# First x rows, w1 and w2 rounded to bf16 by the loading DMA; whole form rows stored; three plain h pairs

## The chip, the cores and the metric

One core of a Trainium2 chip runs the whole computation. Its engines are named as in the profile: PE (TensorE, matmuls) with PEld (its weight loads), DVE (VectorE), ACT (ScalarE), POOL (GpSimd) and SP (SyncE, which here only issues DMAs; the profile calls its queue SPq). SP and POOL each issue DMAs to a queue of their own: q1 (hardware_dynamic) is SP's, q0 (software_dynamic) is POOL's; both are served by the same 16 DMA engines. The metric is the device time of one execution in microseconds; lower is better.

## The reference

```python
y = np.matmul(x, w1) + b1          # x: 16x512x768, w1: 768x3072
y = 0.5 * y * (1.0 + erf(y / np.sqrt(2.0)))
out = np.matmul(y, w2)             # w2: 3072x768, all float32 in and out
```

The 16 x 512 rows of x are one list of 8192 rows.

## The kernel before

**Tiling.** The rows are taken in passes of 768 (the last pass has 512); a pass is two halves of 384 rows (`HW`). The inner sizes are K = 768 = 6 blocks of 128 (`KC`), H = 3072 = 24 blocks (`HC`) and N = 768. All matmuls run in bf16 and sum in float32 in PSUM. Blocks h and h + 12 form an "h pair" j (`HP` = 12 pairs).

**Seven products in place of eight.** Both layers use a Strassen-Winograd-like scheme with seven products M1 to M7 on 2x2 blocks. The first layer's matrix operand comes in seven "forms" per h pair: two of them are plain blocks of w1 (M3, M4), five are sums or differences (M1, M5, M2, M6, M7). For one pair they take 7 x 3 x 128 = 2688 bf16 per partition, one `SLOT`. They are too large for SBUF beside the rest, so they lie in a DRAM tile `w1f`, one row of slots per pair, and are read back into a ring of seven slots, `w1t` (`RING` = 7), in every pass after the first. The second layer's seven forms of w2 stay in SBUF (`w2t`, seven places per pair, in the order M3, M4, M1, M5, M2, M6, M7).

**Pass 0** computes the first layer the plain way (`plain(hc, half)`: six matmuls of 384 columns and one gelu on ACT), because the forms of w1 don't exist yet. Pass 1 still does its first `PLAIN` = 4 h pairs in the plain way, 24 matmuls for each, and the other eight with `product1`, 21 matmuls for each. Later passes do all twelve pairs with `product1`.

**Loading.** The inputs are float32. SP loads the first six x tiles (`load_x0`), w1 in nine pieces (`load_w1`, list `W1G`) and w2 in twelve (`load_w2`, list `W2P`) into scraps of other tiles (`xft`, `st`, `ot`, `tt`, the end of `w2t`). DVE, ACT and POOL then round each to bf16: `cast_x0` and `cast_w1`. `turn_x0` transposes an x tile on PE and copies it from PSUM into `xt`. `make_w2(j, part)` reads the float32 scrap of pair j: DVE writes five sums into `w2t`, POOL copies the two plain blocks. The lists `ORDER` and `USER` interleave loads and casts so that a scrap is free before it is loaded again.

**Order.** Every instruction is issued through `inorder`, so each engine runs its own list in the order of the program; engines meet through semaphores. In pass 0 the list of DVE after the first layer is: sums of gelu rows for the second layer (`gsum`), between them the sums of the last three w2 pairs (`late_w2`), and then the evacuations of the second layer (`evacuate`, lines 117-135). PE runs through M3 and M4 of the second layer pair by pair for all three row blocks, then M1, M5, M2, M7, M6 of each block (`rest`).

**Forms.** `make_w1` makes the five sums for one pair on DVE (four instructions) into a scrap in `tt` or `st` and SP stores them to `w1f`. `store_raw` stores the two plain blocks of all pairs in two DMAs with pieces of 768 bytes. Pass 0 calls `make_w1` in `forms(1)` after some of the second layer's products; pass 1 calls the rest between its plain pairs, two after each. `load_raw_slots` issues the first loads of the ring as soon as the raw w1 below a slot is used up.

**Tiles used twice.** `tt` is both the place of form scraps and the place to which `product1` evacuates (`tj = tt[:, j % 2]`); `xft` holds sums of x (`sum_x`). The x of the next pass comes through POOL's queue (`prepare_x`: a DMA that rounds to bf16, into one of three `xb` buffers) and a transposing DMA on SP's queue.

Of the kernel before, what the change touches and what calls it, by code (L numbers as in the profile page):

```python
# [12 lines left out]
P = 128  # L13
# [17 lines left out]
def kernel(  # L31
# [23 lines left out]
    PLAIN = 4  # L55
# [47 lines left out]
    def add(dst, a, b):  # L103
        inorder(nc.vector.tensor_tensor(out=dst, in0=a, in1=b, op=ALU.add))  # L104
# [147 lines left out]

    def make_w2(j, part):
        s = s2[j]
        b11, b12, b21, b22 = s[:, 0, :NB], s[:, 0, NB:], s[:, 1, :NB], s[:, 1, NB:]
        f = w2t[:, j]
        if part == 0:
            sub(f[:, WF["M3"], :], b22, b12)
            sub(f[:, WF["M4"], :], b11, b21)
            copy("pool", f[:, WF["M5"], :], b22)  # L260
            copy("pool", f[:, WF["M2"], :], b11)
        else:
            add(f[:, WF["M1"], :], b11, b22)
            add(f[:, WF["M6"]:WF["M7"] + 1, :], s[:, :, :NB], s[:, :, NB:])

    def raw(j):
        return w1t[:, j * RAW:(j + 1) * RAW].rearrange("p (hh kh c) -> p hh kh c", hh=2, kh=2)

    stf = st[:].rearrange("p a b c -> p (a b c)")
    ttb = tt[:].rearrange("p a b c -> p (a b c)").bitcast(BF16)  # L270
    made = 0
    FORMS0 = 7

    def make_w1():
        nonlocal made
        j = (made + PLAIN) % HP
        a = raw(j)
        area, n = (ttb, made % 3) if made < FORMS0 or made >= FORMS0 + 4 else (stf, made - FORMS0)
        made += 1
        s = area[:, n * 5 * KH * P:(n + 1) * 5 * KH * P].rearrange("p (f c) -> p f c", f=5)  # L280
        add(s[:, 0, :], a[:, 0, 0, :], a[:, 1, 1, :])
        add(s[:, 1:3, :], a[:, :, 0, :], a[:, :, 1, :])
        sub(s[:, 3, :], a[:, 0, 0, :], a[:, 1, 0, :])
        sub(s[:, 4, :], a[:, 1, 1, :], a[:, 0, 1, :])
        dma(nc.sync, out=w1f[j].rearrange("p (f c) -> p f c", f=7)[:, 2:, :], in_=s)

    def store_raw(f, blk):
        src = w1t[:, :HP * RAW].rearrange("p (j b c) -> p j b c", j=HP, b=4)[:, :, blk, :]
        dma(nc.sync, out=w1f[:].rearrange("j p (f c) -> p j f c", f=7)[:, :, f, :], in_=src)

    def plain(hc, half):
        pool, nm = ((ps_x, "psx"), (ps_y, "psy"))[half]
        hh, j = divmod(hc, HP)
        py = pool.tile([P, 512], FP32, name=nm)
        for kc in range(KC):
            o = ((j * 2 + hh) * KC + kc) * P
            inorder(nc.tensor.matmul(out=py[:, :HW], lhsT=w1t[:, o:o + P], rhs=xt[:, kc, half, :],  # L297
                                     start=(kc == 0), stop=(kc == KC - 1)))
        inorder(nc.scalar.activation(out=g[:, hc, half, :], in_=py[:, :HW], func=ACTF.Gelu,  # L299
                                     bias=b1t[:, hc:hc + 1], scale=1.0))  # L300
# [14 lines left out]
    late = w2t[:].rearrange("p a b c -> p (a b c)")[:, 8 * 7 * NB:]  # L315
    xftf = xft[:].rearrange("p a b c -> p (a b c)")

    def words(ap, first, count):
        return ap[:, 2 * first:2 * (first + count)].bitcast(FP32)

    otw = ot[:].rearrange("p a b -> p (a b)")
    ttw = tt[:].rearrange("p a b c -> p (a b c)")
    W1G = [(0, 1, words(xftf, 0, 768)), (1, 2, words(xftf, 768, 1536)), (12, 3, words(stf, 0, 2304)),
           (3, 3, otw), (15, 3, words(late, 0, 2304)), (6, 3, words(xftf, 0, 2304)),
           (18, 3, words(stf, 0, 2304)), (9, 3, otw), (21, 3, words(xftf, 0, 2304))]
    pa, pb, pc = ttw[:, :1536], ttw[:, 1536:3072], words(stf, 2304, 1536)
    pd, pe = words(xftf, 0, 1536), otw[:, :1536]
    W2P = [words(late, 2304, 1536), words(late, 3840, 1536), pa, pb, pc, pa, pb, pe, pc, pd, pa, pb]

    def load_x0(n):  # L330
        s = words(late, n * K, K)
        dma(nc.sync, out=s, in_=xf[n * P:(n + 1) * P, :])
        return s

    def cast_x0(s, engine):
        xb = xbp.tile([P, K], BF16, name="xb")
        copy(engine, xb[:], s)
        return xb

    def turn_x0(n, xb, e1):  # L340
        pt = ps_z.tile([P, KC, P], BF16, name="psz")
        for kc in range(KC):
            inorder(nc.tensor.transpose(out=pt[:, kc, :], in_=xb[:, kc * P:(kc + 1) * P], identity=ident[:]))  # L343
        half, c0 = place(HW, n)
        copy(e1, xt[:, :, half, c0:c0 + P], pt[:])

    s1, s2 = {}, {}

    def load_w1(n):
        h0, nh, area = W1G[n]  # L350
        s1[n] = area.rearrange("p (kc c) -> p kc c", kc=KC)
        dma(nc.sync, out=s1[n], in_=w1r[:, :, h0 * P:(h0 + nh) * P])

    def cast_w1(n, engines):
        h0, nh, _ = W1G[n]
        for i in range(nh):
            hh, j = divmod(h0 + i, HP)
            o = (j * 2 + hh) * KC * P
            copy(engines[i], w1t[:, o:o + KC * P].rearrange("p (kc c) -> p kc c", kc=KC),
                 s1[n][:, :, i * P:(i + 1) * P])  # L360

    def load_w2(j):
        s2[j] = W2P[j].rearrange("p (hh n) -> p hh n", hh=2)
        dma(nc.sync, out=s2[j], in_=w2r[:, j, :, :])

    def group(n):
        h0, nh, _ = W1G[n]
        for hc in range(h0, h0 + nh):
            plain(hc, 0)
            plain(hc, 1)  # L370


    xs = [load_x0(n) for n in range(3)]
    load_w1(0)
    b1s = words(stf, 2304, P)[:HC, :]
    dma(nc.sync, out=b1s, in_=b1.rearrange("(hc p) -> hc p", p=P))
    load_w1(1)
    xs += [load_x0(n) for n in range(3, 6)]
    load_w1(2)
    load_w1(3)  # L380
    ident32 = words(stf, 2432, P)
    make_identity(nc, ident32)
    nc.gpsimd.tensor_copy(out=ident[:], in_=ident32)
    xbs = [cast_x0(xs[n], e) for n, e in enumerate(("dve", "act", "dve"))]
    for n, e in enumerate(("act", "dve", "dve")):
        turn_x0(n, xbs[n], e)
        busy(1)
    cast_w1(0, ["act"])
    tb = ps_z.tile([P, 512], FP32, name="psz")
    inorder(nc.tensor.transpose(out=tb[:, :HC], in_=b1s, identity=ident32[:HC, :HC]))  # L390
    copy("act", b1t[:], tb[:, :HC])
    cast_w1(1, ["dve", "pool"])
    for n in range(3):
        plain(n, 0)
    for n, e in enumerate(("dve", "act", "dve")):
        turn_x0(n + 3, cast_x0(xs[n + 3], "act" if n == 1 else "dve"), e)
    for n in range(3):
        plain(n, 1)

    pool3 = ["pool"] * 3  # L400
    engines = {2: ["pool", "dve", "pool"], 3: ["dve", "pool", "dve"], 4: ["pool", "dve", "pool"]}
    ORDER = ["a4", "b0", "a5", "b1", "b2", "a6", "b3", "a7", "b4", "a8",
             "b5", "b6", "b7", "b8", "b9", "b10", "b11"]
    USER = {"a5": "a1", "a6": "a2", "a7": "a3", "a8": "a5", "b5": "b2", "b6": "b3", "b7": "a7",
            "b8": "b4", "b9": "a8", "b10": "b5", "b11": "b6"}
    waiting = ["a2", "a3"]

    def process(what):
        k = int(what[1:])
        if what[0] == "a":  # L410
            cast_w1(k, engines.get(k, pool3))
        elif k < 9:
            make_w2(k, 0)
            make_w2(k, 1)

    for what in ORDER:
        while USER.get(what) in waiting:
            process(waiting.pop(0))
        (load_w1 if what[0] == "a" else load_w2)(int(what[1:]))
        waiting.append(what)  # L420
    for what in waiting:
        process(what)
    for n in range(2, 9):
        group(n)
    late_w2 = [lambda: make_w2(9, 0), lambda: make_w2(10, 0), lambda: make_w2(11, 0),
               lambda: make_w2(9, 1), lambda: make_w2(10, 1), lambda: make_w2(11, 1)]
    store_raw(WF["M3"], 0)
    store_raw(WF["M4"], 3)


    for p, (r0, w) in enumerate(pairs):
# [43 lines left out]
        else:  # L475
            js = list(range(PLAIN if p == 1 else 0, HP))
            if p == 1:
                for j in range(PLAIN):
                    for hc in (j, HP + j):
                        plain(hc, 0)  # L480
                        plain(hc, 1)
                    for _ in range(2):
                        if made < HP:
                            make_w1()
                    load_raw_slots(j + 1)
                for k in range(5):
                    sum_x(k, w)
# [33 lines left out]
        def load_raw_slots(plain_done=0):  # L521
            nonlocal nload
            free = 0
            while nload < RING:
                k = (nload + FIRST) % RING
                need = {j for j in range(HP) if j * RAW < (k + 1) * SLOT and (j + 1) * RAW > k * SLOT}
# [29 lines left out]
        if ns > 2:  # L556
# [6 lines left out]
            rest(2, "M7", forms(1) if later else xsums(4))  # L563
# [31 lines left out]
```

## Time and profile before

| what | value |
|---|---|
| median of 3 runs | 901.2 us (901.19 to 901.29) |
| profiled execution | 901.6 us |
| its span, first to last instruction | 899.8 us |
| PE busy | 890.4 us, 99% of the span, 5556 matmuls |
| DVE / ACT / POOL busy | 619.8 / 379.4 / 102.8 us |
| granted TensorE clock | 0.999 |
| first layer of pass 0 runs without a gap from | 16.36 us |
| its last matmul ends, second layer begins | about 60.2 us |
| plain pairs of pass 1 | 101.70 to 117.30 us |

The profiled execution is 0.4 us above the median, and 1.8 us of it lie outside the span. "Busy" counts an engine's instructions only; a matmul's duration includes its time in the pipeline, so the pace of matmuls is read from how far apart they start: twelve of 384 columns take 1.95 us, 0.1625 us each. A name like `tt<-w1t` reads "writes tt, reads w1t"; x12 means that twelve instructions are merged.

### The profile page before, as it was taken

How to read it: one execution, taken by the hardware profiler on the slowest of the kernel's cores; microseconds unless marked ns; L12 is line 12 of the kernel's file. 1: busy time of each engine (PE TensorE's matmuls, PEld its weight loads, DVE VectorE, ACT ScalarE, POOL GpSimd, SP SyncE). 2: the span in 40 equal slices, each digit the busy share in tenths (PEclk: the TensorE clock that was granted, in tenths of full speed). 3: DMA queues.
4: the chain of work that ended last, by engine and by line, in shares of the span. 5: the costliest groups of instructions: out<-in, count | busy, mean ns of one | idle time of the engine just before them, and what ended most of it. 6: DMA issues, size and time to landing. Idle time of an engine off the chain costs nothing.

```text
span 899.8 us, 14338 instructions
## 1 busy us (share of the span) xinstructions
PE 890.4 (99%) x5556; PEld 542.7 (60%) x5556; DVE 619.8 (69%) x1080; ACT 379.4 (42%) x600; POOL 102.8 (11%) x167
## 2 busy tenths in 40 slices
PE   7999999999999999999999999999999999999998
PEld 4656666666666666666666666666666666666774
DVE  3798956677667676766776676767667766767665
ACT  4541264057207603740572176038306711850460
POOL 2871100010110011000101100110001011000000
PEclk9999999999999999999999999999999999999999
DMA  9998986356717554672557266545726682662411
GB/s 327 385 350 174 316 312 192 106 154 206 185 60 205 200 133 113 213 183 90 171 198 176 74 208 202 133 118 194 180 88 184 204 157 87 205 201 88 153 37 71
DMA packets 92952, 158.23 MB, mean 176 GB/s; under 512 B 50877, under 2 KB 68309, under 8 KB 92885
## 3 DMA queue, kind: packets, MB, share of 16 engines
q1 hardware_dynamic: 79732, 122.32, 43.3%
q0 software_dynamic: 13152, 35.00, 15.2%
q8 instruction: 43, 0.70, 0.3%
q14 instruction: 25, 0.20, 0.1%
HBM read 123.88 MB, written 33.42 MB: 175 GB/s over the span
## 4 chain that ended last, share of the span: by engine, by line
PE 98%; DMA 1%; SPq 0%; ACT 0%; DVE 0%; issue 0%
PE psx L203 21%; PE psy L203 21%; PE psx L160 18%; PE psy L160 18%; PE psz L203 7%; PE psz L160 6%; PE psy L297 3%; PE psx L297 3%; DMA xft<-in_w_dram 1%; SPq L73 0%; ACT g L299 0%; PE psz L343 0%; ACT xb L97 0%; DVE w1t L99 0%; DVE xt L99 0%
## 5 line engine op out<-in xcount | busy, mean ns | idle before, releaser
L160 PEld LDWEIGHTS <-w1t 128*128 128x128 bf16 x2436 | 238.4, 98 | 144.4
L203 PEld LDWEIGHTS <-st 128*128 128x128 bf16 x1920 | 187.9, 98 | 124.1
L97 ACT COPY x<-psx 128x384 f32<-128x384 f32 (+1 forms) x148 | 67.5, 457 | 265.2 <-PE psx L203 191.2
L160 PE MATMUL psx<-xft,w1t 128*128 128x384 bf16 (+1 forms) x696 | 147.2, 320 | 0.0
L160 PE MATMUL psy<-xft,w1t 128*128 128x384 bf16 (+1 forms) x696 | 147.2, 320 | 0.0
L168 ACT ACTIVATE g<-tt,b1t 128x768 bf16<-128x768 f32 (+1 forms) x116 | 106.0, 914 | 80.5 <-DVE tt L107 80.5
L203 PE MATMUL psx<-w2t,st 128*128 128x384 bf16 x768 | 135.3, 326 | 0.0
L203 PE MATMUL psy<-w2t,st 128*128 128x384 bf16 x768 | 135.3, 326 | 0.0
L104 DVE TENSOR_TENSOR q<-x,psy 128x384 f32<-128x384 f32 (+1 forms) x148 | 80.2, 543 | 53.7 <-ACT x L97 38.6
L172 ACT ACTIVATE g<-tt,b1t 128x768 bf16<-128x768 f32 (+1 forms) x116 | 105.8, 912 | 22.8 <-DVE tt L107 22.8
L97 ACT COPY z<-psz 128x384 f32<-128x384 f32 (+1 forms) x148 | 69.3, 468 | 98.7 <-PE psz L203 55.8
L203 PEld LDWEIGHTS <-g 128*128 128x128 bf16 x768 | 75.1, 98 | 49.8 <-issue 0.6
L107 DVE TENSOR_TENSOR tt<-z,psx 128x384 f32<-128x384 f32 (+1 forms) x116 | 62.7, 541 | 51.0 <-PE psx L160 51.0
L107 DVE TENSOR_TENSOR tt<-z,psy 128x384 f32<-128x384 f32 (+1 forms) x116 | 62.6, 540 | 45.1 <-PE psy L160 45.1
L104 DVE TENSOR_TENSOR st<-g 128x1536 bf16<-128x1536 bf16 (+2 forms) x116 | 92.6, 812 | 0.0
L73 POOL DMA_DIRECT2D xb<-in_x_dram x58 | 31.2, 549 | 438.7 <-DMA xt<-xb 435.9
L203 PE MATMUL psx<-w2t,g 128*128 128x384 bf16 x384 | 74.2, 326 | 0.0
L160 PE MATMUL psz<-xft,w1t 128*128 128x384 bf16 (+1 forms) x348 | 73.6, 320 | 0.0
L160 PE MATMUL psy<-xt,w1t 128*128 128x384 bf16 (+1 forms) x348 | 73.6, 320 | 0.0
L160 PE MATMUL psx<-xt,w1t 128*128 128x384 bf16 (+1 forms) x348 | 73.6, 320 | 0.0
L203 PE MATMUL psy<-w2t,g 128*128 128x384 bf16 x384 | 72.9, 326 | 0.3 <-ACT g L299 0.3
L203 PE MATMUL psz<-w2t,st 128*128 128x384 bf16 x384 | 67.6, 326 | 0.0
(64 smaller groups left out, 593.6 us busy)
## 6 DMA issues: line engine op xcount, KB each, us to landing
w1t<-w1f SPq DMA_DIRECT2D x116, 672.0 KB, 4.0
out_dram<-ot POOLq DMA_DIRECT2D x60, 384.0 KB, 2.6
xb<-in_x_dram POOLq DMA_DIRECT2D x58, 192.0 KB, 4.6
tt<-in_w_dram SPq DMA_DIRECT2D x6, 768.0 KB, 10.0
w1f<-tt SPq DMA_DIRECT2D x8, 480.0 KB, 2.8
w2t<-in_x_dram SPq DMA_DIRECT2D x6, 384.0 KB, 6.7
st<-in_w_dram SPq DMA_DIRECT2D x2, 1152.0 KB, 11.8
ot<-in_w_dram SPq DMA_DIRECT2D x2, 1152.0 KB, 13.1
```

The source lines that it names most:

```text
L73: inorder(queue.dma_start(out=out, in_=in_))
L97: inorder(nc.scalar.copy(out=dst, in_=src))
L104: inorder(nc.vector.tensor_tensor(out=dst, in0=a, in1=b, op=ALU.add))
L107: inorder(nc.vector.tensor_tensor(out=dst, in0=a, in1=b, op=ALU.subtract))
L160: inorder(nc.tensor.matmul(out=ps[:, :w], lhsT=forms[:, WF[m], kc, :], rhs=moving1(m, kc, w), start=(kc == 0 and m in ("M1", "M3", "M4")), ...
L168: inorder(nc.scalar.activation(out=g[:, j, :, :w], in_=tj[:, 0:2, :w], func=ACTF.Gelu, bias=b1t[:, j:j + 1], scale=1.0))
L172: inorder(nc.scalar.activation(out=g[:, HP + j, :, :w], in_=tj[:, 2:4, :w], func=ACTF.Gelu, bias=b1t[:, HP + j:HP + j + 1], scale=1.0))
L203: inorder(nc.tensor.matmul(out=ps[:, :NB], lhsT=lhs, rhs=w2t[:, j, WF[m], :], start=(j == 0 and m in ("M1", "M3", "M4")), stop=(j == HP - ...
L297: inorder(nc.tensor.matmul(out=py[:, :HW], lhsT=w1t[:, o:o + P], rhs=xt[:, kc, half, :], start=(kc == 0), stop=(kc == KC - 1)))
```

## The change

1. x tiles 0 to 5, w1 and w2 are loaded by DMAs on POOL's queue that round float32 to bf16 on the way. The x tiles land in `st`, w1 lands where the matmuls read it, w2's four blocks of a pair land in places 2 to 5 of `w2t`. All casts of x and w1 on DVE, ACT and POOL go, and so do POOL's copies of w2.
2. w1 is loaded in eight groups of three h blocks (`GRP`), group 0 in two halves of K. The issue order on POOL is x0, x1, (the identity matrix), x2, the halves of group 0, x3 to x5, groups 1 to 3, w2 of pairs 0-2, groups 4 to 6, w2 of pairs 3-5, group 7, w2 of pairs 6-8, w2 of pairs 9-11; one w2 load is two DMAs.
3. `make_w2` makes five sums of 384 bf16 on DVE, partly in place: M7, then M1 over the place of b21, then M6 over that of b12.
4. `make_w1` puts all seven forms into one scrap of a whole slot (in `tt`, `xft` or `st`): one ACT copy for the two plain blocks, four DVE instructions for the sums, and one DMA of 672 KB. `store_raw` goes. Three calls stand in pass 0's first layer (with the last w1 group), six in its second layer, three in pass 1, one after each plain pair.
5. `PLAIN` is 3, so pass 1 has three plain pairs and nine in `product1`.

```diff
-    PLAIN = 4
+    PLAIN = 3
+    GRP = 3 * KC * P
+    def load_w2(j, n):
+        for hh, f in ((0, 4), (1, 2)):
+            dma(nc.gpsimd, out=w2t[:, j:j + n, f:f + 2, :].rearrange("p j f n -> p j (f n)"),
+                in_=w2r[:, j:j + n, hh, :])
     def make_w2(j, part):
-        s = s2[j]
-        b11, b12, b21, b22 = s[:, 0, :NB], s[:, 0, NB:], s[:, 1, :NB], s[:, 1, NB:]
         f = w2t[:, j]
+        b21, b22, b11, b12 = f[:, 2, :], f[:, 3, :], f[:, 4, :], f[:, 5, :]
         if part == 0:
             sub(f[:, WF["M3"], :], b22, b12)
             sub(f[:, WF["M4"], :], b11, b21)
-            copy("pool", f[:, WF["M5"], :], b22)
-            copy("pool", f[:, WF["M2"], :], b11)
         else:
+            add(f[:, WF["M7"], :], b21, b22)
             add(f[:, WF["M1"], :], b11, b22)
-            add(f[:, WF["M6"]:WF["M7"] + 1, :], s[:, :, :NB], s[:, :, NB:])
+            add(f[:, WF["M6"], :], b11, b12)
+    def load_w1(gi, k0=0, k1=KC):
+        c0 = (gi % 2 * HP + gi // 2 * 3) * P
+        dma(nc.gpsimd, out=w1_group(gi)[:, k0:k1, :], in_=w1r[:, k0:k1, c0:c0 + 3 * P])
     def make_w1():
...
-        area, n = (ttb, made % 3) if made < FORMS0 or made >= FORMS0 + 4 else (stf, made - FORMS0)
+        if made < HP - PLAIN:
+            area, o = ((ttb, 0), (ttb, 3072), (xftf, 0), (xftf, SLOT))[made % 4]
+        else:
+            area, o = ((stf, 0), (stf, SLOT), (ttb, 3072))[made - HP + PLAIN]
         made += 1
...
+        copy("act", s[:, 0:2], a[:, 0:4:3])
+        add(s[:, 2], a[:, 0], a[:, 3])
+        add(s[:, 3:5], a[:, 0:4:2], a[:, 1:4:2])
+        sub(s[:, 5], a[:, 0], a[:, 2])
+        sub(s[:, 6], a[:, 3], a[:, 1])
+        dma(nc.sync, out=w1f[j], in_=area[:, o:o + SLOT])
-    def store_raw(f, blk):
...
     def load_x0(n):
-        s = words(late, n * K, K)
-        dma(nc.sync, out=s, in_=xf[n * P:(n + 1) * P, :])
+        dma(nc.gpsimd, out=xb0[:, n, :], in_=xf[n * P:(n + 1) * P, :])
...
+    load_x0(0)
+    load_x0(1)
+    ident32 = words(stf, 2432, P)
+    make_identity(nc, ident32)
+    copy("pool", ident[:], ident32)
+    load_x0(2)
+    load_w1(0, 0, KH)
+    load_w1(0, KH, KC)
+    for n in range(3, 6):
+        load_x0(n)
+    for gi in range(1, 4):
+        load_w1(gi)
+    load_w2(0, 3)
+    for gi in range(4, 7):
+        load_w1(gi)
+    load_w2(3, 3)
+    load_w1(7)
+    load_w2(6, 3)
+    load_w2(9, 3)
...
+    for k0 in (0, KH):
+        for n in range(3):
+            plain(n, 0, k0, k0 + KH)
+    for n, e in enumerate(("dve", "dve", "dve")):
+        turn_x0(n + 3, e)
+    for n in range(3):
+        plain(n, 1)
+    for k in range(9):
+        make_w2(k, 0)
+        make_w2(k, 1)
+    for gi in range(1, 8):
+        for n in range(3):
+            hc = gi % 2 * HP + gi // 2 * 3 + n
             plain(hc, 0)
             plain(hc, 1)
+            if gi == 7:
+                make_w1()
...
-                    for _ in range(2):
-                        if made < HP:
-                            make_w1()
+                    if made < HP:
+                        make_w1()
...
-            rest(2, "M7", forms(1) if later else xsums(4))
+            rest(2, "M7", () if later else xsums(4))
```

## The prediction

> **What bounds the kernel now.** I read the page first (busy times, chain), then busy time by stretch, then the order of time where PE is not busy.
>
> ```profile
> span 899.8 us, 14338 instructions
> PE 890.4 (99%) x5556; PEld 542.7 (60%) x5556; DVE 619.8 (69%) x1080; ACT 379.4 (42%) x600; POOL 102.8 (11%) x167
> PE 98%; DMA 1%; SPq 0%; ACT 0%; DVE 0%; issue 0%
> ```
>
> The chain is PE for 98%. So a change pays only by fewer matmuls or by filling PE's gaps, and any new wait of PE costs in full. The gaps, by stretch (columns: stretch, its length, then busy us of PE, PEld, DVE, ACT, POOL; granted clock, DMA share, GB/s):
>
> ```profile
> 10.00:15.00 5.00, 2.96 (x24) 1.65 (x22) 2.20 (x4) 2.46 (x4) 1.22 (x1) 1.00 1.04 386
> 15.00:20.00 5.00, 4.35 (x35) 2.75 (x34) 1.12 (x2) 2.46 (x4) 1.99 (x2) 1.00 1.06 374
> 60.00:70.00 10.00, 9.66 (x60) 5.69 (x59) 10.00 (x16) 0.63 (x2) 3.81 (x5) 1.00 1.00 276
> ```
>
> After 20 us PE loses 0.34 us at 60 us and, at the very end, what the last evacuations cost. DVE is full at 60-70, so it is nearly the bound there. The start, in order of time (start, length, engine):
>
> ```profile
> 14.32 0.55 DVE L99 CAST xb<-w2t 128x768 bf16<-128x768 f32 x1
> 14.86 0.84 PE L343 MATMUL psz<-ident,xb 128*128 128x128 bf16 x12 [1.06 <-ACT xb L97]
> 15.74 0.56 DVE L99 COPY xt<-psz 128x768 bf16<-128x768 bf16 x1 [0.88 <-PE psz L343]
> 16.36 0.82 PE L297 MATMUL psy<-xt,w1t 128*128 128x384 bf16 x4 [0.65 <-DVE xt L99]
> ```
>
> Cast, transpose, copy: only then, at 16.36, does PE run on without a gap. What the new loads cost is read from the two kinds of queue, rounding DMAs on POOL's queue (windows of 6.6 us from 153.4, and of 12 us from 63) and float32 loads on SP's (10 us from 40):
>
> ```profile
> q0 software_dynamic: 432, 0.59, 60.6%
> ...
> q0 software_dynamic: 432, 0.59, 30.0%
> ...
> q1 hardware_dynamic: 1723, 3.90, 103.2%
> 103.28 1.63 POOL L73 DMA_DIRECT2D xb<-in_x_dram  x3
> ```
>
> **Change, part 1: fewer matmuls.** One h pair goes from 24 to 21 matmuls: 3 x 0.1625 = **-0.49 us**, on the path.
>
> **Part 2: the start.** POOL's first x DMA can issue where POOL works now, at 0.73. A rounding DMA of 128 rows takes 0.54 us to issue; its data lands 2.7 to 4.6 us after issue in an unloaded stretch (three at 235.5). The pace of its data: 60.6% x 16 x 6.6 us over 432 packets (384 of them rows, 3072 bytes read) is 148 ns a packet; in the window 63 to 75 it is 30.0% x 16 x 12 / 432 = 133. SP's loads moved 3.90 MB in 10 us, 390 GB/s or 126 ns for 3072 bytes on one engine. So rounding runs at 0.85 to 0.95 of that: 332 to 370 GB/s of float32 read; I take 351. No row shows rounding in rows of 1536 bytes (w1); SP's loads keep 387 GB/s with such rows among them (20 to 30 us), so I use the same pace. Issue of 384 or 768 runs isn't shown either: between 0.54 us (all fixed) and 1.6 and 3.3 us (all by the run); both are below the 1.7 and 3.4 us that the data takes, so either way the data sets the pace.
> x0 to x2 end at about 5.9 (x2 is issued at 2.8, after the identity's 0.9 us, and needs 3.1). The two halves of w1 group 0 and x3 to x5, 2.36 MB, follow: 6.7 us, 12.6, landed 12.9. Then six transposes 0.45, one copy 0.56 and the hops between: PE starts half 1 at **14.3, 2.1 us earlier** than 16.36 (bounds: 1.4 at 332 GB/s with a 0.3 us later first issue, 2.7 at 390). x3 and x4 need no cast and are copied meanwhile.
> From there PE needs a w1 group each 36 x 0.1625 = 5.85 us; one takes 3.4 us, a w2 load 6.7. Group 1 lands at 16.3 (needed 17.2), group 4 at 33.3 (34.8), group 7 at 50.6 (52.3). PE is fed, with 1 us in hand.
>
> **Part 3: casts that go.** POOL's casts and DVE's and ACT's lie beside PE after 20 us: worth nothing. DVE's sums of w2 become bf16; the like rows `tt<-w1t` start 0.27 us apart (four in 1.27). A w2 pair is five of them, one with a wait on the one before it: 1.5 us.
>
> **Part 4: w2 at the end of pass 0's first layer.** PE leaves that layer at 14.3 + 43.9 + the old 0.4 = 58.6 (60.2 before). w2 of pairs 6-8 is the last load but one: after 5.9 us come x3 to x5, all of w1 and six of the eight w2 DMAs, 1.2 + 9.4 + 7.1 = 17.7 MB; at 351 GB/s it has landed at 56.3. DVE, in its order: three pairs 4.5 (60.8); three `make_w1`, new here, 4.0 (64.8); `gsum` M1 0.87; then three times a late pair's part 0 (0.54) with `gsum` M5, M2 between (69.0; w2 of 9-11 landed at 63); part 1, nine sums, 2.8 (71.8); `gsum` M7, M6 1.8 (73.6); q 0.55 (74.2). PE wants pair 11 at 69.4, the last M1 form at 71.8 and M2's bank, which q frees, at 74.1. So the DVE chain ends when PE comes. Before, M2 ran from 76.19; now from 74.4: of 2.1 us **-1.8 stays**. Any delay of that load is paid in full: at 332 GB/s it lands at 59.2, 2.9 later, and -1.8 becomes +1.1; at 370 it is earlier and all 2.1 stay.
> ACT's three copies here (0.8 each, as its 128x768 copies) fit: one comes after every second gelu, ACT idles 0.39 us after each, and a half has three PSUM buffers to wait in; without that room each would cost PE up to 0.8.
>
> **Part 5: the stores.** The bytes to `w1f` are the same: 12 x 672 KB for 2 x 1152 and 12 x 480. On SP's queue three stores now stand ahead of the transposes of pass 1's x; they are issued by 65, the transposes began at 69.93, and pass 1 needs them at 100: hidden by the second layer of pass 0, 35 us; past that each us late is one of PE. POOL's queue has all loads ahead of the same x, landed at about 66: hidden likewise.
> In pass 1 a wait is added. The last plain pair ends at P (117.30 before). The rows there:
>
> ```profile
> 117.50 0.58 ACT L299 ACTIVATE g<-psy,b1t 128x384 bf16<-128x384 f32 x1 [0.40 <-PE psy L297]
> 117.99 0.48 ACT L97 COPY x<-psx 128x384 f32<-128x384 f32 x1
> 119.45 0.56 DVE L107 TENSOR_TENSOR tt<-psx,q 128x384 f32<-128x384 f32 x1 [0.35 <-PE psx L160]
> ```
>
> The twelfth `make_w1` has its ACT copy behind the gelu of that pair, P+0.7 to P+1.5. Its scrap is the second half of `tt`, which the first `product1` (j = 3, odd) evacuates into. So: ACT's copy x of M4 comes after it, P+1.9 instead of P+1.2; M5 writes that bank and waits 0.4 us; SP's store goes at P+1.5 and lands about 3.2 us later (480 KB stores: 2.5 to 2.8; 192 KB more at SP's pace 0.5); only at P+4.7 may DVE evacuate M5 (P+2.15 before), done P+5.3. Queued behind it on DVE are M2's evacuation, the next q and M7's. PE's M7 writes the same bank and stood at P+3.9: it starts at P+5.4, **+1.5** (bounds 0.8 with the store landing in 2.5, 2.3 with 4.0). The backlog on DVE, three of 0.5 us, clears before PE's next M7. Before, all sums of w1 were done at 108.75 and the store long landed.
>
> **Sum**: -0.5 - 1.8 + 1.5 = -0.8, with a little for small waits not seen: **-0.6 us**. On the profiled execution (899.8 span, 901.6 whole) that is 901.0; it stood 0.4 above the median, so 900.6.
>
> **Rules of the skill, weighed.** POOL's three issues at 103.28 took 0.54 us each while DVE ran sums without a break (102.37 to 108.75). The Trainium skill, "SBUF — State Buffer", section "SBUF: two separate sides", warns against just this change: descriptors of POOL's DMAs are written by POOL itself, a DVE instruction in a two-port mode locks it out, and a DMA of 620 ns took 3100. By it, 2.5 us more for each of the 23 loads, an estimate from that page, would bring the load of pairs 6-8 far past 56 and the sum to tens of us slower; the row shows no such lock for two-input sums, and the changed start has few other DVE instructions. On issue the same skill's "DMA: Bandwidth & Descriptors", "Anatomy of one DMA", says that many descriptors can be emitted before their number costs anything; that is the lower end, 0.54, and leaves the sum as it is.
>
> **Rivals.**
> A. The rounding loads are slower than 351 GB/s, and w2 comes late: slower than before. Each us that the load of pairs 6-8 is late beyond 56 is a us of PE. It decides from 57.1, where -0.5 - 1.8 + 0.8 + 1.5 is nought; 332 GB/s gives -0.5 + 1.1 + 1.5 = +2.1, 903.3; 315 GB/s (0.81) lands at 62.1, +5.0, 906. For it: 148 ns, w1's short runs. Against it: the 133 ns, and that SP's loads at full queue overlap (103%).
> B. The store's wait in pass 1 is not there or short (ACT's copy earlier, the store landing at once), and the loads keep 370 or more: -0.5, -2.1 to -2.7, and 0 to 0.5: 898.0 to 899.1. Against it: the order of ACT's list.
> C. POOL's issue becomes the bound. 8 w1 groups and 6 w2 DMAs until pairs 6-8 are 11 group issues; with 5 us for the rest they exceed 56 us if a group takes over 4.6 us (6 ns a run; 0.54/128 is 4.2). At 8.4 ns: 76 us, landing 80, about +23: 924.
> D. The first POOL DMA starts 2 us late: start gain gone, w2 2 us later: -0.5 + 0.2 + 1.5 = +1.2: 902.4.
>
> **How the numbers follow.** 0.2% of 901.2, 1.8 us, is about what a measurement of this kernel tells from none. My case: 0.38, 899.4 to 902.5. A 0.23; B 0.25; C 0.06; D 0.08. Faster is B: 0.25. Slower is most of A, C, part of D and the upper end of mine: 0.36. Same: 0.39. The range from 898.2 leaves out little of B; up to 906.0 it leaves out C and the end of A: under 2 in 10.
>
> **What would show it.** Right: 5553 matmuls; PE's first unbroken plain matmul near 14.3; M2 of the first block near 74.4; in the waits a DVE `tt` evacuation waiting for DMA `w1f<-tt`, and PE waiting 1 to 2 us for DVE at the first `product1`; POOL issues of w1 below 3.3 us. Wrong: PE waiting for `w1t<-in_w1`, DVE for `w2t` past 57, POOL issues above 4.6 us.

## The result and the profile after

The changed kernel takes 905.5 us (median of 5 runs, 904.1 to 905.8) beside 901.2 for the kernel before (5 runs on the same chip). The ratio is 1.0041 with a 95% interval of 1.0026 to 1.0056: slower by 0.4%. The prediction said 900.6 and a range of 898.2 to 906.0; the time lies inside the range but at its far end, and on the wrong side of no change. The profiled execution took 905.73 us, its span is 903.9, against 899.8 before: 4.1 us more.

The page of the changed kernel, busy times and the chain that ended last:

```profile
span 903.9 us, 14283 instructions
PE 891.5 (99%) x5553; PEld 542.7 (60%) x5553; DVE 596.4 (66%) x1089; ACT 385.5 (43%) x608; POOL 81.4 (9%) x148
...
PE 94%; DMA 3%; DVE 1%; POOL 1%; issue 0%; ACT 0%; DVEq 0%; POOLq 0%
```

PE does three matmuls fewer and is yet busy 1.1 us longer. So some matmuls ran slower, and not only waits were added. The chain is no longer PE alone: DMA has 3% of it.

Busy time by stretch (stretch, its length, busy us of PE, PEld, DVE, ACT, POOL; granted clock, DMA share, GB/s):

```profile
10.00:15.00 5.00, 3.12 (x30) 1.89 (x28) 1.02 (x2) 1.55 (x3) 2.78 (x5) 1.00 1.20 196
15.00:20.00 5.00, 4.35 (x30) 2.59 (x27) 0.56 (x1) 1.82 (x4) 1.46 (x2) 1.00 1.31 203
20.00:50.00 30.00, 30.00 (x187) 18.06 (x185) 8.77 (x30) 17.91 (x31) 6.28 (x9) 1.00 1.23 207
60.00:70.00 10.00, 9.66 (x61) 5.72 (x59) 8.94 (x21) 1.19 (x2) 1.59 (x3) 1.00 1.00 236
70.00:100.00 30.00, 29.36 (x181) 17.56 (x180) 21.73 (x44) 7.16 (x12) 2.17 (x4) 1.00 0.81 248
100.00:110.00 10.00, 9.95 (x62) 6.00 (x62) 9.45 (x23) 4.69 (x9) 2.70 (x5) 1.00 0.96 334
110.00:120.00 10.00, 7.92 (x48) 4.55 (x47) 0.68 (x2) 5.95 (x11) 0.00 (x0) 1.00 1.06 347
120.00:130.00 10.00, 9.52 (x49) 5.27 (x49) 6.98 (x14) 5.42 (x8) 0.00 (x0) 0.83 0.54 179
```

The last two stretches in the kernel before:

```profile
110.00:120.00 10.00, 10.00 (x63) 6.05 (x62) 3.28 (x6) 5.85 (x12) 0.00 (x0) 1.00 1.06 359
120.00:130.00 10.00, 10.00 (x64) 5.99 (x62) 7.32 (x15) 6.90 (x11) 0.00 (x0) 1.00 0.86 336
```

Four things are to be seen. The start gained next to nothing. From 20 to 50 us PE is full, so the loads feed it. Between 70 and 100 us 0.64 us is idle, where PE was full before (30.00 of 30.00). And the loss lies in 110 to 130 us: 2.1 us of PE idle, then ten microseconds in which the clock granted was 0.83 and only 49 matmul records stand where the same stretch had 64 before.

The start, first POOL's rows and then PE's (start, length, engine, then in brackets the idle time ahead and what ended it):

```profile
1.25 1.23 POOL L74 DMA_DIRECT2D st<-in_x_dram  x2 [0.81 <-POOLq L542]
3.35 0.55 POOL L74 DMA_DIRECT2D st<-in_x_dram  x1
...
7.26 0.51 PE L343 MATMUL psz<-ident,st 128*128 128x128 bf16 x6 [0.59 <-DMA st<-in_x_dram]
11.82 1.64 PE L313 MATMUL psx<-xt,w1t 128*128 128x384 bf16 x9 [1.47 <-DMA w1t<-in_w_dram]
14.66 0.51 PE L343 MATMUL psz<-ident,st 128*128 128x128 bf16 x6 [0.42 <-DMA st<-in_x_dram]
15.82 3.08 PE L313 MATMUL psy<-xt,w1t 128*128 128x384 bf16 x18 [0.65 <-DVE xt L100]
```

PE runs without a gap from 15.82, not from 14.3: a gain of 0.54 us on 16.36. And pass 1, where the three plain pairs end at P = 113.69:

```profile
114.37 0.82 ACT L98 COPY tt<-w1t 128x768 bf16<-128x768 bf16 x1
115.22 0.32 SPq L74 DMA_DIRECT2D w1f<-tt  x1
119.87 0.56 DVE L108 TENSOR_TENSOR tt<-psx,q 128x384 f32<-128x384 f32 x1 [3.71 <-DMA w1f<-tt]
120.48 0.65 PE L161 MATMUL psx<-xft,w1t 128*128 128x384 bf16 x3 [2.26 <-DVE tt L108]
120.97 0.65 PE L161 MATMUL psx<-xt,w1t 128*128 128x384 bf16 x3
121.45 0.87 PE L161 MATMUL psx<-xft,w1t 128*128 128x384 bf16 x3
122.12 1.16 PE L161 MATMUL psy<-xft,w1t 128*128 128x384 bf16 x3
123.08 1.16 PE L161 MATMUL psy<-xt,w1t 128*128 128x384 bf16 x3
```

In the kernel before, the first product's M4 and M7, with P = 117.30:

```profile
117.30 0.65 PE L160 MATMUL psx<-xft,w1t 128*128 128x384 bf16 x3
121.20 0.65 PE L160 MATMUL psx<-xft,w1t 128*128 128x384 bf16 x3
```

In the changed kernel the last form store is issued at 115.22. DVE may not overwrite its scrap in `tt` until it has landed, at about 119.7; M7 of the first product (120.48) then stands at P + 6.8 instead of P + 3.9. Behind it the groups of three matmuls start 0.96 us apart (122.12 to 123.08) where 0.4875 is normal: half the clock. The next product's M7 comes 5.1 us after, at 125.57, against the normal 3.41.

The account, against the kernel before: start -0.54; three matmuls -0.49; a gap of PE at 99 us +0.85 (by the starts of the matmuls; below); the store's wait +2.9; half clock +1.7. The sum is +4.4. The last twelve matmuls of the kernel do start 4.37 us later than before (897.98 for 893.61); the span grows by only 4.1, since what follows them is 0.3 us shorter.

### The profile page after: what moved, and what is told of

Its sections match the earlier page's. It is cut to its first block, busy times and chain, and to the rows that moved or that the text cites. A ratio compares the mean times of both kernels' runs of the same rounds, so it can differ in the third digit from the quotient of the medians.

```text
span 903.9 us, 14283 instructions
## 1 busy us (share of the span) xinstructions
PE 891.5 (99%) x5553; PEld 542.7 (60%) x5553; DVE 596.4 (66%) x1089; ACT 385.5 (43%) x608; POOL 81.4 (9%) x148
## 4 chain that ended last, share of the span: by engine, by line
PE 94%; DMA 3%; DVE 1%; POOL 1%; issue 0%; ACT 0%; DVEq 0%; POOLq 0%
PE psx L204 20%; PE psy L204 20%; PE psy L161 18%; PE psx L161 18%; PE psz L204 6%; PE psz L161 6%; PE psy L313 3%; PE psx L313 2%; DMA out_dram<-ot 1%; DMA st<-in_x_dram 1%; DMA w1f<-st 1%; DMA w1f<-tt 1%; DVE ot L108 0%; POOL st L74 0%; DVE st L105 0%
## 5 line engine op out<-in xcount | busy, mean ns | idle before, releaser
L161 PEld LDWEIGHTS <-w1t 128*128 128x128 bf16 x2457 | 240.9, 98 | 149.8 <-issue 4.8
L161 PE MATMUL psy<-xft,w1t 128*128 128x384 bf16 (+1 forms) x702 | 149.5, 322 | 0.0
L108 DVE TENSOR_TENSOR tt<-z,psx 128x384 f32<-128x384 f32 (+1 forms) x117 | 63.2, 541 | 50.1 <-PE psx L161 50.1
L108 DVE TENSOR_TENSOR tt<-psx,q 128x384 f32<-128x384 f32 (+1 forms) x117 | 63.5, 543 | 6.7 <-DMA w1f<-tt 3.7
```

Of the source, the lines that this page charges most:

```text
L161: inorder(nc.tensor.matmul(out=ps[:, :w], lhsT=forms[:, WF[m], kc, :], rhs=moving1(m, kc, w), start=(kc == 0 and m in ("M1", "M3", "M4")), ...
```

## The experiments

Each ratio is to the kernel before on the same chip: it took 901.8 us beside the first four runs, 901.6 beside the next four and 901.7 beside the last two.

### Issue the last store early

If the store is late because ACT's copy stands behind the gelus, moving the copy to GpSimd cures it.

```diff
-        copy("act", s[:, 0:2], a[:, 0:4:3])
+        copy("act" if made <= HP - PLAIN else "pool", s[:, 0:2], a[:, 0:4:3])
```

> The changed kernel with one thing moved: the copy of the two plain blocks for the last three form rows (pass 1) runs on POOL in place of ACT. Theory S (PE's loss in pass 1 is the wait for the last form store out of tt, which is issued only after ACT's copy behind the last gelu): the last w1f<-tt store is issued before 110 us in place of 115.2, DVE's first tt evacuation waits for no DMA, M7 of the first product starts 3.9 us after the first M4 (6.8 now), and the clock stays at 1.0 after it: 905.5 - 2.9 - 1.7 = 901. Rival V (DVE itself is late there, or PE waits for something else): PE still starts M7 more than 5 us after the first M4 and the time stays above 904.

Measured: 904.87 us, ratio to the kernel before 1.0030 (1.0018 to 1.0042). Rows of SP, DVE and PE:

```profile
108.55 0.32 SPq L74 DMA_DIRECT2D w1f<-tt  x1
...
119.50 0.56 DVE L108 TENSOR_TENSOR tt<-psx,q 128x384 f32<-128x384 f32 x1 [4.50 <-DMA w1f<-tt]
120.11 0.66 PE L161 MATMUL psx<-xft,w1t 128*128 128x384 bf16 x3 [2.85 <-DVE tt L108]
```

The copy did what was wanted: the store goes out 6.7 us earlier than in the changed kernel, at 108.55. It lands hardly earlier all the same, 10.8 us after issue (4.5 in the changed kernel), and M7 still stands 6.91 us behind the first M4 (113.20). So the order of ACT's list, on which the prediction had built the wait, is not by itself the cause. What stays: the DMA engines are busy without a break there (share 1.00 from 100 to 110 us, 1.07 from 110 to 115, 1.05 from 115 to 120), with two ring loads, three form stores, output stores and the next x. The reading from here on is that a store issued into this backlog waits its turn; the runs with more and with fewer loads ahead of it test that.

### Keep PE busy while it waits

```diff
+                if p == 1 and s == 2:
+                    px = bank(ts[2], "M4")
+                    for _ in range(14):
+                        inorder(nc.tensor.matmul(out=px[:, :w], lhsT=ident[:], rhs=xft[:, 0, 0, :w],
+                                                 start=True, stop=True, skip_group_check=True))
```

(It stands in the loop over `s`.)

> The changed kernel with 14 extra matmuls of 384 columns, 2.3 us, put on PE just ahead of the first product's M7, into a PSUM bank that is free then; their values are overwritten and reach no output. The store wait is left as it is. Theory C (the granted clock falls to half after PE has idled 2.3 us, and costs some 1.7 us over the next 3.4): M7 starts as late as before, 6.8 us after the first M4, but the clock stays at 1.0, the next M7 comes 3.4 us later (5.1 now), and the time is about 905.7 - 1.7 = 904.0. Rival D (the slow matmuls have another cause, such as what DVE or DMA do there): the extra matmuls change nothing after M7 and the time stays at 905.5.

Measured: 903.37 us, ratio 1.0012 (1.0002 to 1.0023). PE's rows in order of time:

```profile
116.76 2.44 PE L461 MATMUL psx<-xft,ident 128*128 128x384 bf16 x14
119.15 0.65 PE L161 MATMUL psx<-xft,w1t 128*128 128x384 bf16 x3
...
122.56 0.65 PE L161 MATMUL psx<-xft,w1t 128*128 128x384 bf16 x3
```

M7 still stands 6.76 us behind M4 (112.39), so the store's wait is all there. But the next M7 follows after 3.41 us, and the clock is 1.00 in every window. The half clock is the price of PE standing still, and not of what stands behind it. It is worth about 1.7 us (5.09 to 3.41 between the two M7). The median fell by 2.15; the trace also lacks the gap at 99 us and starts 0.46 us earlier (unbroken from 15.36), which the 14 matmuls can't have brought.

### More traffic ahead of the last store

```diff
                 make_w1()
-                load_raw_slots()
+                if made == HP - PLAIN:
+                    load_raw_slots()
```

> The changed kernel with the first loads of the w1t ring issued only after the ninth form row is stored (about 101 us) in place of three times from 83 us on. Theory Q (POOL's output stores at 90.8 and 92.5 wait behind SP's ring loads, so that the ot buffer comes free late and PE waits 0.7 to 0.85 us for the M2 evacuation at 99.4): the output stores land in under 5 us, M6 of the third block follows without a gap, pass 1 begins 0.8 us earlier, 904.7. Rival W (it is the form stores themselves that hold them up): the output store of 90.8 still lands after more than 7 us and PE waits as before. Either way the loads now fall on the form stores of pass 1, and the store wait there may grow by up to 2 us.

Measured: 909.84 us, ratio 1.0089 (1.0064 to 1.0115). This was aimed at the gap at 99 us: in the changed kernel an output store that POOL's queue issued at 90.77 landed only near 99.3, and M6 of the third block had to wait for its buffer:

```profile
100.05 2.11 PE L204 MATMUL psy<-w2t,st 128*128 128x384 bf16 x12 [0.69 <-DVE ot L108]
```

With the ring loads moved behind it, that gap is gone. But the loads now stand ahead of the last store, which takes 9.0 us from issue to landing in place of 4.5; DVE waits 8.13 us for it in place of 3.71, PE 6.68:

```profile
123.79 0.56 DVE L108 TENSOR_TENSOR tt<-psx,q 128x384 f32<-128x384 f32 x1 [8.13 <-DMA w1f<-tt]
```

The landing follows the traffic. The half clock behind this longer wait cost more, too: the next M7 comes 6.08 us after the first (3.41 is normal), 2.7 us. The gap at 99 us itself is not settled by this run: in the two runs above, which did not touch these loads, it is 0.13 us and nothing, and 0.66 us in another (all by the starts of the matmuls).

### The identity later

```diff
     load_x0(1)
+    load_x0(2)
+    load_w1(0, 0, KH)
     ident32 = words(stf, 2432, P)
     make_identity(nc, ident32)
     copy("pool", ident[:], ident32)
-    load_x0(2)
-    load_w1(0, 0, KH)
```

> The changed kernel with POOL making the identity matrix after the issue of x2 and of the first half of w1 group 0, in place of after x1. Theory I (the loads come late because POOL issues them late: DMA engines idle before 4 us): x2 and all behind it land about 0.9 us earlier, x5 at 13.7, and PE runs without a gap from 14.9 in place of 15.8: 904.6. Rival R (the pace of the data, or of the slowest DMA engine, sets x5's landing and the issue does not): x5 still lands near 14.6 and PE starts at 15.8.

Measured: 904.3 us, ratio 1.0022 (1.0010 to 1.0034). The start got worse in its trace, not better:

```profile
9.61 4.78 PE L313 MATMUL psx<-xt,w1t 128*128 128x384 bf16 x18 [0.93 <-DMA w1t<-in_w_dram]
...
16.52 1.78 PE L313 MATMUL psy<-xt,w1t 128*128 128x384 bf16 x10 [0.65 <-DVE xt L100]
```

PE's idle time for w1 shrank (0.93 us in place of 2.04), but x2, issued 0.9 us earlier, landed no earlier: its transposes start at 7.78 (7.26 in the changed kernel), and the first w1 matmuls at 9.61 (8.72). That speaks for rival R as far as x2 goes; when x5 landed is hidden behind what follows. The 18 matmuls that take some 3 us at full pace took 4.78 here: half clock once more, 1.7 us, after PE had stood still. So the earlier issue of x2 by itself gained nothing, and the waits of PE at the start can have the same second price as in pass 1. In pass 1 of this trace PE stood still for 2.63 us and the clock stayed at 1.00: not every such gap costs. The median is 1.2 us below the changed kernel's, the trace's span 1.4: no half clock in pass 1 (-1.7) and hardly a gap at 99 us (-0.8) against the later start (+0.7) and a longer wait for the store (+0.4).

### Four plain pairs again

```diff
-    PLAIN = 3
+    PLAIN = 4
...
-    FIRST = -(-PLAIN * RAW // SLOT)
+    FIRST = 4
...
-        if made < HP - PLAIN:
+        if made < 9:
...
-            area, o = ((stf, 0), (stf, SLOT), (ttb, 3072))[made - HP + PLAIN]
+            area, o = ((stf, 0), (stf, SLOT), (ttb, 3072))[made - 9]
```

> The changed kernel with four plain h pairs instead of three; all else as changed. The order of the stores stays: the twelfth and last form store (which reads the scrap in tt that the first product's evacuation overwrites) is still issued in the third plain block of pass 1, but a fourth plain block of 3.9 us now lies between it and the products. Theory B (the last store lands late because the DMA engines work off a backlog without a break, so that its landing hardly depends on when it is issued, and the three-pair kernel comes to the evacuation 3.7 us too early): the landing stays near 119 to 120, the evacuation comes 3.9 us later, its wait for DMA w1f<-tt is under 0.5 us (3.71 in the changed kernel), TensorE stands still for less than 0.5 us ahead of the first product's M7, no half clock follows; 905.5 - 2.9 - 1.7 + 0.5 = 901.4 us. Rival L (the landing follows the work, since what keeps the engines busy moves along): the wait stays above 2 us and the time is 905.5 to 906.5.

Measured: 900.99 us, ratio 0.9992 (0.9983 to 1.0002). DVE's row of the first evacuation:

```profile
119.19 0.56 DVE L108 TENSOR_TENSOR tt<-psx,q 128x384 f32<-128x384 f32 x1 [0.35 <-PE psx L161]
```

DVE waits for PE there, as before the change, and not for the store. The store was issued at 114.66 and took 4.1 us, so it had landed at 118.8. The edit does a second thing that the text of the expectation does not name: with four plain pairs the first product is j = 4, an even one, which evacuates into the other half of `tt`; the scrap is first overwritten by the second product, at 122.11. One pair more in the plain way costs 0.49 us of matmuls, and the time falls by 4.5 us all the same.

### The last scrap in the other half of tt

```diff
-            area, o = ((stf, 0), (stf, SLOT), (ttb, 3072))[made - HP + PLAIN]
+            area, o = ((stf, 0), (stf, SLOT), (ttb, 0))[made - HP + PLAIN]
```

> The changed kernel, with the last form pair built in the half of tt that the second product evacuates into, not the first (three plain pairs as in the change). Theory B: the first evacuation has nothing to wait for; the second product's first evacuation, 3.4 us later (near 119.6 on the changed kernel's clock), meets a store that lands near 119.8, so it waits 0 to 0.5 us; TensorE goes through, no half clock; 905.5 - 2.9 - 1.7 = 900.9 us. Rival M (the wait only moves: the landing comes later or the next thing that is late, the ring's form rows for the pairs behind, takes its place): a wait of 2 us or more at the second product or a wait of TensorE on DMA w1t, and 903.5 to 905.5 us.

Measured: 900.91 us, ratio 0.9995 (0.9985 to 1.0004). Three plain pairs, the same traffic, the same order of issue; one number in the code. The second product's evacuation now meets the store, 3.4 us later:

```profile
115.25 0.32 SPq L74 DMA_DIRECT2D w1f<-tt  x1
...
119.64 0.56 DVE L108 TENSOR_TENSOR tt<-psx,q 128x384 f32<-128x384 f32 x1 [0.31 <-DMA w1f<-tt]
```

The store is issued when it was in the changed kernel (115.25 for 115.22) and lands when it did (4.3 us after issue, 4.5 there). Only the instruction that has to wait for it has moved. M7 of the first product stands at P + 4.4 (118.09 behind 113.72) and the clock stays at 1.00, so by the traces 2.4 us of wait and 1.7 of half clock are gone; the 0.5 that stays is M5's wait for ACT's copy, which the longer wait had covered. The last matmuls start 4.07 us earlier than in the changed kernel; the medians differ by 4.6, the ratios by 0.46%, 4.1 us.

### Fewer loads ahead of the last store

```diff
-            while nload < RING:
+            while nload < (RING if made == HP else 3):
```

(beside the copies on GpSimd of the first run)

> The earlier run with the last three copies of the plain blocks on GpSimd (904.87, the last store issued at 108.55 and landed near 119.4), and beside it the fourth and fifth ring load of form rows put behind the last form store, not ahead of it. The scrap is as in the change. Theory B (backlog): two transfers of 672 KB less ahead of the last store, at some 3.5 us each by the time that the stores beside them took: it lands 3 to 7 us earlier, by 116.5 at the latest, the evacuation does not wait, no half clock: 904.9 - 2.85 - 1.7 = 900.3, up to 901.5 if some wait is left. Rival K (the three stores go one behind the other on their queue at their own pace, whatever else is there): landing 119 to 119.5, time 904.5 to 905. Rival R (the postponed loads come too late for the pairs 6 and 7): TensorE waits for DMA w1t<-w1f behind the second or third product, 902 us or more.

Measured: 901.12 us, ratio 0.9994 (0.9985 to 1.0003). By the time theory B holds, by the landing only in part. The store was issued at 109.77 and took 8.2 us where it took 10.8 with the two loads ahead of it: 2.6 us less, not 3 to 7, and it landed near 118.0, not by 116.5. (That the loads behind it, which share the engines with it, took the rest is likely, but no run shows it.) PE waits 0.19 us:

```profile
118.66 0.65 PE L161 MATMUL psx<-xft,w1t 128*128 128x384 bf16 x3 [0.19 <-DVE tt L108]
```

Pass 1 came late in that trace: its unbroken stretch began at 17.39, 1.6 us behind the changed kernel's, with 18 matmuls at half clock (4.78 us) behind a wait of 2.25 us for w1. That is not what made the wait small. The stores move with pass 1, and in the last two runs below, which have the same pass 1 but 2.1 and 2.6 us earlier, the store took 8.0 and 8.1 us and M7 stood 4.06 and 4.12 us behind the first M4, for 4.25 here.

### Three x tiles by SP

```diff
     def load_x0(n):
+        if n < 3:
+            s = words(late, n * K, K)
+            dma(nc.sync, out=s, in_=xf[n * P:(n + 1) * P, :])
+            copy(("dve", "act", "dve")[n], xb0[:, n, :], s)
+            return
         dma(nc.gpsimd, out=xb0[:, n, :], in_=xf[n * P:(n + 1) * P, :])
```

(with both halves of w1's group 0 at the head of POOL's queue, the load of b1 behind x2 on SP's, and the scrap of the run before last; `late` is the end of `w2t`, as in the kernel before)

> As the run with the other half of tt, and the first three row tiles of x are loaded as float32 by SyncE's queue and rounded by VectorE and ScalarE, as in the kernel before; rows 3 to 5, w1 and w2 stay rounded by the DMA, w1's first group now at the head of GpSimd's queue. Theory S (the start was gained only 0.5 us because GpSimd's first issue is at 1.25 us and its loads come slowly up to speed, one queue serving all): x's first tiles land near 3.3 to 5 us, w1's first half near 7, and TensorE runs without a break from 14.3 to 14.8 in place of 15.8: 1.0 to 1.5 us off the run with the other half of tt. Rival T (the bytes of x and of w1's first group set it, whichever queue brings them): without a break from 15.5 to 16.2, the same time within 0.3 us.

Measured: 901.69 us (899.1 to 903.1), ratio 0.9996 (0.9984 to 1.0008). Neither theory is met by the trace: the unbroken stretch began at 16.58, but w1 was there in time and the 18 matmuls took 4.65 us, behind a wait of PE of 1.60 us for the cast of x2. The spread of the times, 4 us, is the widest of the four runs from four plain pairs on. With the scrap of the run before last the store took 6.1 us here for 4.3 there, and M7 of the second product came 0.56 us late: that scrap leaves little to spare.

### The waits at the start filled

```diff
         turn_x0(n, e)
-        busy(1)
+        busy(2)
...
+    busy(3)
     for k0 in (0, KH):
         for n in range(3):
             plain(n, 0, k0, k0 + KH)
+        if k0 == 0:
+            busy(5)
```

(beside the edits of the run with fewer loads; `busy(n)` is n matmuls into a bank that nobody reads)

> The run with two ring loads fewer ahead of the last store (901.1; its trace began the unbroken stretch of TensorE at 17.39, since 18 matmuls of the first groups ran at half clock, 4.78 us, after TensorE had waited 2.25 us for w1), and beside it 11 more matmuls into the unused scratch bank while TensorE waits for x and w1 at the start. Theory C (a wait of TensorE near 2 us costs a stretch at half clock at the start as in pass 1): no half clock ahead of 20 us, the unbroken stretch begins at 15.8 or before, 1.0 to 1.6 us off that trace and 0.3 to 1.5 off the median, since only part of the executions will have had it: 899.6 to 900.8. Rival T (the landing of x5 and of w1 sets the start, and the half clock ran in time that was waited for anyway): the same 901.1 within 0.4 us, and a start at 15.8 to 17.4 as before.

Measured: 901.08 us, ratio 0.9994 (0.9985 to 1.0002). In the trace the clock is 1.00 throughout and the unbroken stretch begins at 15.33, as theory C says; but the median ratio is that of the run without these matmuls, as rival T says. Without them four of ten executions had a mean clock of 0.998, with them all eleven had 0.999 or 1.000, and yet their times spread from 900.0 to 902.1. So something besides the clock varies from execution to execution; these were not traced, and it stays open.

### Both

```diff
         turn_x0(n, e)
-        busy(1)
+        busy((2, 6, 2)[n])
...
+    busy(2)
     for k0 in (0, KH):
```

(beside the three x tiles by SP, the copies on GpSimd and the fewer loads; the scrap is the change's)

> The same pass 1 as the run beside it, with the first three row tiles of x by SyncE's queue in float32 (as in the run that had its unbroken stretch from 16.58, with 18 matmuls at half clock in 4.65 us), and 9 more scratch matmuls in the waits at the start. Theory C with S: the 18 matmuls take 2.9 to 3.1 us, the unbroken stretch begins at 14.6 to 15.3, and the time is 898.3 to 899.7. Rival T: the stretch begins at 15.8 or later whatever the clock, since x3 to x5 or w1 land then; 900.3 to 901.2.

Measured: 900.44 us (899.7 to 900.9, 11 runs), ratio 0.9986 (0.9977 to 0.9995). This is the one version that is faster than the kernel before by more than its interval, by 0.14%; it beats the changed kernel by about 0.5%. PE's rows at the start:

```profile
9.24 3.09 PE L313 MATMUL psx<-xt,w1t 128*128 128x384 bf16 x18
12.16 0.83 PE L350 MATMUL psz<-ident,st 128*128 128x128 bf16 x12
13.31 0.49 PE L350 MATMUL psz<-ident,st 128*128 128x128 bf16 x6 [0.31 <-DVE xt L100]
14.46 3.08 PE L313 MATMUL psy<-xt,w1t 128*128 128x384 bf16 x18 [0.65 <-DVE xt L100]
```

No row of PE waits for a DMA any more, and PE runs on from 14.46, near the start that the prediction had worked out for the change itself. The median, 900.44, stayed above the 898.3 to 899.7 expected. Its span, 898.0, is 1.8 below that of the kernel before, where the start (-1.9) and three matmuls (-0.5) make 2.4; by the starts of the matmuls a gap at 98 us (0.33) and one ahead of the first product's M7 (0.22) give the rest back.

## Why the prediction was wrong

**Part 1, right.** 5553 matmuls, three fewer.

**Part 2, the start: mechanism right, sum mis-sized.** POOL's first issue stands at 1.25 us, not at 0.73: what the trace of before shows at 0.73 is not the moment at which its queue can start. x2 was issued at 3.35 (2.8 expected) and had landed by 7.26 (5.9 expected); the 2.36 MB behind it took 7.4 us, 319 GB/s, for the 6.7 at 351. Of the 1.5 us missed, 1.4 lie ahead of x2; the slower pace behind it was mostly made up by a shorter end (1.16 us from x5's landing to 15.82, where 1.4 was allowed). The last run comes near 14.3, at 14.46, but by other means: the first tiles on SP's queue beside POOL's, and PE kept at work. With all loads on POOL's queue the earliest start of any trace here is 15.33, with PE kept at work too. (A slip without consequence: group 7 of w1 lands at 50.1 by the prediction's own pace, not at 50.6.)

**Issue and pace afterwards, better than priced.** Issues of 384 and 768 runs took 0.74 to 0.84 us, near the lower end taken (0.54) and far from 1.6 and 3.3. On this point "DMA: Bandwidth & Descriptors", "Anatomy of one DMA" of the Trainium skill was right: six times the runs of an x tile cost 0.3 us more. The lock-out of POOL by DVE's two-port modes that the same skill's "SBUF — State Buffer", section "SBUF: two separate sides", warns of is not seen: no such issue took over 0.84 us, and two that fell into a stretch in which DVE ran sums without a break (29.25 and 32.15, in 29.05 to 33.5) took 0.77 and 0.76. Whether any DVE instruction here ran in such a mode no row tells. From 20 to 50 us the rounding DMAs alone:

```profile
q0 software_dynamic: 5946, 6.18, 122.5%
```

6.18 MB in 30 us is 206 GB/s of bf16 written, or 412 of float32 read: above the range of 332 to 370, and above the 390 of SP's plain loads. Rivals A and C are ruled out: the load of pairs 6 to 8 landed at about 52 and not 56.3.

**Part 4, right in kind.** No late w2; M2 of the first block ran from 75.64, that is 0.55 earlier than 76.19, which is the start's gain passed on. The -1.8 was the start's error and no new one.

**Part 5, the term that failed.** The place was right to the instruction: the first evacuation of `product1` waits for the twelfth store, and the store goes at P + 1.5 as worked out. The term was put at +1.5 us; it measured +4.6, 2.9 of wait and 1.7 of half clock. Two steps of it failed.

First, the landing. 3.2 us after issue was worked out from stores that took 2.5 to 2.8; it took 4.5, and M7 stood at P + 6.8 for P + 5.4. The reason given, ACT's copy behind the gelu, was not what set the landing: with the store issued 6.7 us earlier DVE could go on only 0.4 us sooner. The lower bound, 0.8 us, came from the same stores, which were issued in a quieter stretch (DMA share 0.83 from 83 to 100 us); for the 4.0 us behind the upper one, 2.3, no row was given. The trace of before showed how crowded pass 1 is. Its form stores (engine, count, size, median us from issue to landing):

```profile
w1f<-tt SPq DMA_DIRECT2D x8, 480.0 KB, 2.8
w1f<-st SPq DMA_DIRECT2D x4, 480.0 KB, 11.4
```

The four of the second row, issued between its plain pairs (103.8 to 108.3 us), took 9.9 to 12.1 us each; the DMA share there was 1.01 (103 to 110 us; 1.09 from 110 to 115 us, 1.04 from 115 to 120). A store of 672 KB into that stretch could not be priced at 3.2 from them. The last form store of before went out behind them:

```profile
110.76 1.17 SPq L73 DMA_DIRECT2D w1f<-tt  x1
123.33 0.56 DVE L107 TENSOR_TENSOR tt<-psx,q 128x384 f32<-128x384 f32 x1 [0.89 <-PE psy L160]
```

"The store long landed" was not shown either: the profile has no landing for that store. Its scrap lay in the half of `tt` that the second product evacuates into, so the first evacuation, at 119.45, was no test of it; the first instruction to overwrite it is the second row, 12.6 us after the issue. (That row's idle time may have been the store's; PE lost nothing by it.) In the changed kernel DVE stood ready to overwrite the scrap about 1 us after the issue. One pair less, a later issue and the other half of `tt` took the cover away together, and gave back 0.49.

Second, a price that no term held: PE standing still for 2.3 us was followed by 3.4 us at half clock, 1.7 us more. The trace of before has no such gap after the start, so it showed no such row; the gap was in my sum, its consequence not.

**Rivals.** A and C fell with the pace and the issue of the loads. B had the loads right, even faster than it asked, but the wait that it thought away was the largest term. D named the right trouble at the start (the first POOL DMA late, 0.5 instead of 2 us). None had the backlog. The gap of 0.85 us at 99 us was in nobody's list; its cause is not settled. That the time still fell inside the stated range is owed to the width of the range, drawn for slow loads, and not to the mechanism.

## What to carry to other kernels

Price a transfer by the stretch into which it is issued, not by like transfers in quiet stretches: here, where the DMA share was 1 and above, the landing went with what stood ahead of the store, and issuing it 6.7 us earlier bought 0.4. When a change shortens the work that covers a landing, look for who is the first to read or overwrite the buffer; moving that reader (here the other half of a scrap) was worth as much as taking back the fourth pair (900.9 and 901.0 us). And a wait of PE of about 2 us can have a second price at half clock, here 1.7 us on top of 2.3.

## What the hardware showed unexpectedly

- After waits of PE of 2.26 and 2.85 us (the changed kernel and the run with the copies on GpSimd) the granted clock was half for about 3.4 us, after one of 6.68 us for about 5.3; 14 matmuls without use in the wait kept it at 1.00. At the start, too, groups of 18 matmuls took 4.65 to 4.78 us instead of 3.1 after waits of 0.5 to 2.25 us just ahead of them, and others before those. A wait of 2.63 us in one trace left the clock at 1.00, so length alone does not decide.
- DMAs that round float32 to bf16 read at 412 GB/s in a steady stretch, faster than the plain float32 loads of the kernel before (390).
- A store of 672 KB took 4.1 to 10.8 us from issue to landing in the crowded stretch, by what stood ahead of it; stores of 480 KB in the kernel before took 9.9 to 12.1 there and 2.5 to 6.1 in the 20 us ahead of it.
